# A mixture of experts on one core: whole rows of the weights, contraction outermost over four (two) PSUM banks, bias products first and on 128 rows

## The chip, the core and the metric

The kernel runs on one core of one Trainium2 chip. TensorE (PE) multiplies matrices into PSUM, VectorE (DVE) and ScalarE (ACT) read and write SBUF and PSUM, GpSimd (POOL) does some elementwise work and issues the gathers and scatters, SyncE (SP) issues the loads of the weights. The metric is the device time of one execution in microseconds.

## The reference

The reference is one transformer block (latent attention beside an indexed sparse attention, then a mixture of 32 experts over 512 tokens with 4 experts for each token), followed by two layers of another block. Only the mixture of experts is changed. It is, cut to its core:

```python
logits = xf @ w_router + b_router
top_val, top_idx = lax.top_k(logits, TOP_K)          # 4 of 32 experts for each of 512 tokens
gates = jax.nn.softmax(top_val, axis=-1)
...
def expert_block(args):                              # xb: rows of one expert
    xb, e = args
    hid = xb @ w_mlp1[e] + b_mlp1[e]                 # [1024] x [1024, 2048]
    glu = jnp.minimum(hid[..., ::2], SWIGLU_LIMIT)
    lin = jnp.clip(hid[..., 1::2], -SWIGLU_LIMIT, SWIGLU_LIMIT)
    act = glu * jax.nn.sigmoid(SWIGLU_ALPHA * glu) * (lin + 1.0)
    return act @ w_mlp2[e] + b_mlp2[e]               # [1024] x [1024, 1024]
...
y = y * slot_gate[:, None]
out = jax.ops.segment_sum(y, slot_tok, num_segments=n + 1)[:n]
```

## The kernel before

The function `moe` does the experts one after another, from about 402 to 1660 us of the span. Each expert takes one block of 96 token rows (`NB`), which a gather on POOL brings (`xg`, L967). An expert's weights are 12 MB, loaded in 12 chunks of 1 MB: `load_to` (L937) asks for a chunk of four 128-row tiles by 512 columns, so that a chunk is four pieces of 2 KB for each of the 128 partitions. Eight chunks are of `w_mlp1` (4 column groups, 2 halves of the contraction), four of `w_mlp2` (2 column groups, 2 halves).

Every chunk is split for accuracy: ACT copies it to `whi` (L85), rounded to the format that PE takes at speed, and DVE forms the rest `wlo` = raw - whi (L86). `mm3` (L88 to L92) then makes three products of each 128-row tile: high rows with whi (L90), high rows with wlo (L91), low rows with whi (L92). `split_to` keeps the splits two chunks ahead of the products (`LA`), `load_to` the loads up to five chunks ahead; there are five raw buffers and three pairs of whi and wlo.

`gemm` (L1025) fills one PSUM bank (96 x 512): 24 products over two chunks, and last one product with `bh` and `sel` that adds the bias (L1035). `bh` holds the high parts of the 32 experts' biases in rows 0 to 31 and the low parts in rows 32 to 63; `sel` picks the expert's two rows. The bank `ph` of the first layer has four buffers, the bank `py` of the second two, and a third pair is shared by transposes (`pt`) and the small products `pq` that give the token numbers of a block. After each `ph` bank `swiglu` (L990) runs four DVE operations on 256 columns (`gl` L995, `ln` L997, L998, `act` L999) and one sigmoid on ACT (`sg` L996). The finished activation is transposed on PE (L986) and split into `ah` and `al` for the second layer, which runs one expert late: an expert's turn has the four `ph` banks of expert e and then the two `py` banks of expert e - 1. `index` finds the next rows, `transposed` makes `xh` and `xl` of them. The result `yo` (L1132, ACT) goes to DRAM by a scatter that adds (L1133, POOL).

The order of the instructions on each engine is set by a scheduler from the written order, so the listings below are of the order that it makes. A further loop (`further_blocks`) for experts with more than 96 tokens runs no turn with these inputs.

Of the kernel before, what the change touches and what calls it, by code (L numbers as in the profile page):

```python
# [73 lines left out]
class K:  # L74
# [19 lines left out]
    def rsqrt_mean(self, pool, ss, n, width):  # L94
        """1 / sqrt(ss / n + EPS) for a [P, width] tile."""
# [44 lines left out]
    def build(self):  # L140
        tc = self.tc
        with ExitStack() as ctx:
            E = ctx.enter_context
            self.cp = E(tc.tile_pool(name="consts", bufs=1))
            self.ps = E(tc.tile_pool(name="ps", bufs=1, space=PSUM))
# [5 lines left out]
            with tc.tile_pool(name="cq", bufs=1, side="right", reuse_waits="tile") as self.cq:  # L151
                self.first_block()
                self.hip = E(tc.tile_pool(name="hip", bufs=2, reuse_waits="tile"))
                self.lop = E(tc.tile_pool(name="lop", bufs=2, reuse_waits="tile"))
                if self.upto >= 2:
                    self.moe()
# [14 lines left out]
    def first_block(self):  # L171
# [9 lines left out]
        with tc.tile_pool(name="pjd", bufs=1, reuse_waits="tile") as pjd:  # L181
# [41 lines left out]
            # parameter columns  # L223
# [11 lines left out]
            # shift and scale of the first norm, in columns; normalised x, transposed  # L235
# [38 lines left out]
            # projections; column starts inside w_in  # L274
# [80 lines left out]
    def modrow(self, w, nk=4):  # L355
        """Two rows (to be summed) of cond @ a [1024, 512] piece of w_ada, given in two halves."""
# [12 lines left out]
    def constants_on_chip(self, tmp):  # L369
        """Shape-only constants of the later parts."""  # L370
# [12 lines left out]
        # routing  # L383
# [18 lines left out]
        self.eye2 = cq.tile([64, NE], F32, name="eye2")  # L402
        DVE.tensor_tensor(self.eye2, self.ident[:64, 0:32], self.ident[:64, 32:64], OP.add)
        # per token and expert: chosen or not, 1 + slot (0 if not chosen), (row in tile, tile's first row, 1, gate in three parts)
# [105 lines left out]
    def latent_inputs(self, pq, cl):  # L510
        """Normalised latents, transposed."""
# [71 lines left out]
    def attention_m(self, k1, cl, ym, sel):  # L583
        """Latent attention; the selection and the other modulation rows run beside it."""
# [6 lines left out]
        with ExitStack() as c:  # L591
# [6 lines left out]
            def mods():  # L598
# [4 lines left out]
                # with biases and gains: (gate 1, shift 2, 1 + scale 2, gate 2) of D each  # L603
# [103 lines left out]
    def attention_d(self, qd, kd, vd, ym, dist, modf):  # L707
        """Selected attention with position biases, last query tile first; output projection, residual,
        second norm and router of each finished tile run beside it."""
# [6 lines left out]
        with ExitStack() as c:  # L716
# [17 lines left out]
            def weights(h, j):  # L734
                """Splits of a quarter of the output projection, in two pieces."""
# [38 lines left out]
            def finish(t):  # L774
                """Residual, second norm; the router works on the row before the norm."""
# [11 lines left out]
            def beside():  # L787
# [9 lines left out]
                # shift and scale of the norm go into the router's bias and weights  # L797
# [31 lines left out]
            def router(t, ss):  # L829
# [13 lines left out]
                # the first four of the sorted logits, ties by the lower expert  # L843
# [16 lines left out]
                # gates  # L860
# [51 lines left out]
    def moe(self):  # L912
# [7 lines left out]
        with ExitStack() as c:  # L920
# [6 lines left out]
            # stream of half chunks of weights, in the order of their use  # L927
            seq = []
            for e in range(NE + 1):
                if e < NE:  # L930
                    seq += [(1, e, n, h) for n in range(4) for h in range(2)]
                if e > 0:
                    seq += [(2, e - 1, n, h) for n in range(2) for h in range(2)]
# [3 lines left out]
            def load_to(i):  # L937
                while nxt[0] <= min(i, len(seq) - 1):
                    w, e, n, h = seq[nxt[0]]
                    raws[nxt[0]] = self.wload((w1 if w == 1 else w2)[e], 4 * h, 4, [(512 * n, 512)])  # L940
# [30 lines left out]
            def index(e):  # L971
# [3 lines left out]
                sel = pm.tile([64, NB], F32R, name="sel", bufs=4)  # L975
                ACT.activation(sel, eye2[:, e:e + 1].to_broadcast([64, NB]), AF.Copy)
                return slots(oh, lambda t: vals[:, t, e, :]) + (sel,)

            def transposed(src, hname, nb):
                h = pm.tile([P, KD, NB], F32R, name=hname + "h", bufs=nb)  # L980
                l = pm.tile([P, KD, NB], F32R, name=hname + "l", bufs=nb)
                for g in range(2):
                    pt = self.pb("pt")
                    for k in range(4):
                        kk = 4 * g + k
                        PE.transpose(pt[:, k * NB:(k + 1) * NB], src[:, kk * P:(kk + 1) * P], ident[:NB, :NB])  # L986
                    self.split(h[:, 4 * g:4 * g + 4, :], l[:, 4 * g:4 * g + 4, :], pt[:, :4 * NB].rearrange("p (k n) -> p k n", k=4))
# [744 lines left out]
```

## Time and profile before

| what | value |
|---|---|
| median of 3 runs | 3064.47 us (3064.34 to 3070.38) |
| profiled execution: span | 3067.3 us |
| PE busy | 2922.3 us (95%) |
| DVE busy | 2197.0 us (72%) |
| ACT busy | 1557.6 us (51%) |
| mixture of experts, from its first gather to its end | about 402 to 1660 us |

The profile gives no other time for the profiled execution than its span, which is 2.8 us (0.1%) above the median. The busy time of PE counts matmuls whose ends are modelled, so 95% says that PE hardly waits, not that it works at its peak. The two layers behind the experts (from about 1720 us) are not touched by the change.

### The profile page before, as it was taken

Reading aid. Unit: us, or ns where it says so; the run is one execution under the profiler, and the core shown is the slowest. Engines: PE = TensorE matmul, PEld = TensorE weight load, DVE = VectorE, ACT = ScalarE, POOL = GpSimd, SP = SyncE. Lnnn points to the kernel's source line nnn. Section 1 sums busy time; section 2 is a strip of 40 time slices with the busy share of each in tenths; the row PEclk is TensorE's granted clock in tenths of the full one; section 3 lists DMA queues with packets and bytes.
Section 4 is the critical chain, followed back from the end, with each engine's and each line's share of the span. In section 5 each row is a group of like instructions: output and inputs, shape, how many; then the busy total and the mean of one; then the engine's idle time right before and its main releaser. Section 6 shows DMA issues by size and latency. Waiting matters only on the chain. (4 is left out here: it accounts for less than half of the span.)

```text
span 3067.3 us, 37240 instructions
## 1 busy us (share of the span) xinstructions
PE 2922.3 (95%) x14328; PEld 2183.2 (71%) x14328; DVE 2197.0 (72%) x3370; ACT 1557.6 (51%) x1861; POOL 228.8 (7%) x139
## 2 busy tenths in 40 slices
PE   6999878999999999999996999999999999999998
PEld 4657745666666666666663877888888877888887
DVE  5797787999999999999997576663334576654333
ACT  5475545777777777777765224542223225442222
POOL 1002221111111111111101000000000000000000
PEclk8999979999999999999998999999999999999999
DMA  7243168999999999999997112123332112033330
GB/s 249 89 152 127 56 238 287 341 345 350 350 350 350 350 349 351 347 352 350 348 351 247 56 42 86 42 97 96 96 96 83 56 42 99 28 106 99 98 96 28
DMA packets 314586, 588.63 MB, mean 192 GB/s; under 512 B 16843, under 2 KB 62262, under 8 KB 314406
## 3 DMA queue, kind: packets, MB, share of 16 engines
q1 hardware_dynamic: 303864, 555.63, 52.2%
q0 software_dynamic: 8416, 29.23, 4.0%
q8 instruction: 114, 1.87, 0.3%
q10 hardware_dynamic: 2126, 1.36, 0.1%
q14 instruction: 66, 0.54, 0.1%
HBM read 566.74 MB, written 19.45 MB: 191 GB/s over the span
## 5 line engine op out<-in xcount | busy, mean ns | idle before, releaser
L86 DVE TENSOR_TENSOR wlo<-raw,whi 128x2048 fp32r<-128x2048 f32 (+2 forms) x525 | 1158.5, 2212 | 401.4 <-ACT whi L85 399.9
L85 ACT ACTIVATE whi<-raw 128x2048 fp32r<-128x2048 f32 (+2 forms) x528 | 976.1, 1855 | 579.9 <-PE pa L92 301.0
L90 PE MATMUL ph<-whi,xh 128*96 128x512 f32 x1024 | 415.2, 405 | 10.1 <-issue 8.5
L91 PE MATMUL ph<-wlo,xh 128*96 128x512 f32 x1024 | 411.7, 402 | 2.5 <-DVE wlo L86 2.4
L92 PE MATMUL ph<-whi,xl 128*96 128x512 f32 x1024 | 405.0, 396 | 0.0
L90 PE MATMUL pa<-hh,whi 128*128 128x512 f32 (+1 forms) x808 | 289.6, 359 | 1.3 <-ACT whi L85 1.3
L91 PE MATMUL pa<-hl,whi 128*128 128x512 f32 (+1 forms) x808 | 288.8, 358 | 0.0
L92 PE MATMUL pa<-hh,wlo 128*128 128x512 f32 (+1 forms) x808 | 287.9, 358 | 0.2 <-DVE wlo L86 0.2
L90 PEld LDWEIGHTS ph<-whi,xh 128*96 128x96 f32 x1024 | 166.0, 162 | 100.5 <-issue 34.2
L91 PEld LDWEIGHTS ph<-wlo,xh 128*96 128x96 f32 x1024 | 166.3, 162 | 67.2 <-DVE wlo L86 4.9
L92 PEld LDWEIGHTS ph<-whi,xl 128*96 128x96 f32 x1024 | 166.9, 163 | 64.2
L90 PE MATMUL py<-whi,ah 128*96 128x512 f32 x512 | 206.7, 404 | 1.2 <-ACT ah L85 1.2
L91 PE MATMUL py<-wlo,ah 128*96 128x512 f32 x512 | 205.0, 400 | 0.3 <-DVE wlo L86 0.3
L92 PE MATMUL py<-whi,al 128*96 128x512 f32 x512 | 200.3, 391 | 0.0
L91 PE MATMUL pa<-wlo,uh 128*128 128x512 f32 x512 | 199.3, 389 | 0.0
L92 PE MATMUL pa<-whi,ul 128*128 128x512 f32 x512 | 199.2, 389 | 0.0
L90 PE MATMUL pa<-whi,uh 128*128 128x512 f32 x512 | 199.1, 389 | 0.0
L90 PEld LDWEIGHTS pa<-hh,whi 128*128 128x128 f32 x808 | 154.0, 191 | 26.1 <-ACT z L567 2.2
L92 PEld LDWEIGHTS pa<-hh,wlo 128*128 128x128 f32 x808 | 153.7, 190 | 22.3 <-DVE wlo L86 0.6
L91 PEld LDWEIGHTS pa<-hl,whi 128*128 128x128 f32 x808 | 153.7, 190 | 21.4
L967 POOL DMA_INDIRECT xg<-h2d,ig x32 | 93.3, 2916 | 634.9 <-issue 516.2
L91 PE MATMUL pa<-wlo,hh 128*128 128x512 f32 (+2 forms) x352 | 133.7, 380 | 3.2 <-DVE wlo L86 3.2
(407 smaller groups left out, 4631.5 us busy)
## 6 DMA issues: line engine op xcount, KB each, us to landing
raw<-in_w_mlp SPq DMA_DIRECT2D x384, 1024.0 KB
raw<-in_w_up SPq DMA_DIRECT2D x32, 1024.0 KB
raw<-in_w_down SPq DMA_DIRECT2D x32, 1024.0 KB
raw<-in_w_in SPq DMA_DIRECT2D x26, 1024.0 KB
raw<-in_w_ada SPq DMA_DIRECT2D x24, 1024.0 KB
raw<-in_w_out SPq DMA_DIRECT2D x8, 1024.0 KB
raw<-in_w_o SPq DMA_DIRECT2D x4, 1024.0 KB
acc<-g SPq DMA_DIRECT2D x5, 512.0 KB
```

The lines of the kernel that those rows point to most:

```text
L85: nc.scalar.activation(hi, src, AF.Copy)
L86: (engine or nc.vector).tensor_tensor(lo, src, hi.bitcast(F32), OP.subtract)
L90: mm(out, lh, rh, start=start, stop=False)
L91: mm(out, lh, rl, start=False, stop=False)
L92: mm(out, ll, rh, start=False, stop=stop)
L967: POOL.indirect_dma_start(out=xg, out_offset=None, in_=self.h2d[:, :], in_offset=bass.IndirectOffsetOnAxis(ap=ig[:, :1], axis=0))
```

## The change

The chunks are cut otherwise. A chunk of `w_mlp1` is now 128 whole rows (one piece of 8 KB for each partition), a chunk of `w_mlp2` is 256 whole rows (two pieces of 4 KB); both are still 1 MB, and an expert still has 8 and 4 of them. `gemm` therefore walks over the contraction in its outer loop and writes four banks (`ph`, 96 x 2048) or two (`py`, 96 x 1024) with each tile. Each of these wide tiles has one buffer (4 + 2 banks), and the last two banks are one wide tile `b`, also with one buffer, for `pq`, the transposes and the count of tokens. The bias product comes first, with `bh` and `sel` on 128 rows (rows 64 to 127 of `bh` are set to zero by POOL). `swiglu` works on 1024 columns and is a generator: `gl`, `sg` and `ln` come after the eighth chunk, the other two steps between chunks of the second layer. `yo` is one operation of 1024 columns. The arithmetic is the same apart from the order of the sums.

```diff
-                seq += [(1, e, n, h) for n in range(4) for h in range(2)]
+                seq += [(1, e, k) for k in range(KD)]
...
-                    raws[nxt[0]] = self.wload((w1 if w == 1 else w2)[e], 4 * h, 4, [(512 * n, 512)])
+                    v = self.rawtile().rearrange("p a b -> p (a b)")
+                    if w == 1:
+                        nc.sync.dma_start(v, w1[e][k * P:(k + 1) * P, :])
+                    else:
+                        nc.sync.dma_start(v.rearrange("p (k n) -> p k n", k=2),
+                                          w2[e][k * P:(k + 2) * P, :].rearrange("(k p) n -> p k n", p=P))
...
-                pq = self.pb("pq")
+                pq = wide_bank("b", 2)
...
-                sel = pm.tile([64, NB], F32R, name="sel", bufs=4)
+                sel = pm.tile([P, NB], F32R, name="sel", bufs=4)
...
+            def swiglu(ph, act):
+                v = ph.rearrange("p (f two) -> p f two", two=2)
+                gl = pm.tile([NB, D], F32, name="gl")
+                ln = pm.tile([NB, D], F32, name="ln")
+                sg = pm.tile([NB, D], F32, name="sg")
+                DVE.tensor_scalar(gl, v[:, :, 0], 7.0, None, OP.min)
+                ACT.activation(sg, gl, AF.Sigmoid, scale=1.702)
+                DVE.tensor_scalar(ln, v[:, :, 1], 7.0, -7.0, OP.min, OP.max)
+                yield
+                DVE.scalar_tensor_tensor(ln, ln, 1.0, gl, OP.add, OP.mult)
+                yield
+                DVE.tensor_tensor(act, ln, sg, OP.mult)
...
-            bh = pm.tile([64, 3 * D], F32R, name="bh")
+            bh = pm.tile([P, 3 * D], F32R, name="bh")
+            POOL.memset(bh[64:P, :].bitcast(F32), 0.0)
...
-            def gemm(out, lh, ll, bias, sel):
+            def gemm(out, lh, ll, b0, sel, kt, between):
...
-                    for k in range(4):
-                        kk = 4 * h + k
-                        self.mm3(out, lh[:, kk, :], ll[:, kk, :], wh[:, k, :], wl[:, k, :], kk == 0, False)
+                    between(i)
+                    for k in range(kt):
+                        kk = kt * i + k
+                        for q, (x, w) in enumerate(((lh, wh), (lh, wl), (ll, wh))):
+                            for n in range(nn):
+                                PE.matmul(out[:, 512 * n:512 * n + 512], x[:, kk, :], w[:, nn * k + n, :],
+                                          start=False, stop=kk == KD - 1 and q == 2)
                     pos += 1
-                PE.matmul(out, sel, bias, start=False, stop=True)
...
+                    def between(i):
+                        if i == 2 and e > 0:
                             st[e - 1]["aT"] = transposed(st[e - 1]["act"], "a", 1)
+                        if i == 4 and e + 2 < NE and e != LOOP:
+                            st[e + 2] = dict(zip(("xg", "isc", "gate", "sel"), index(e + 2)))
+                        if i == 6 and e + 1 < NE:
                             st[e + 1]["x"] = transposed(st[e + 1]["xg"], "x", 2)
+                    gemm(ph, s["x"][0], s["x"][1], 0, s["sel"], 1, between)
+                    glu = swiglu(ph, s["act"])
+                    next(glu)
...
-                    for n in range(2):
-                        py = self.py("py")[:NB, :]
-                        gemm(py, s["aT"][0], s["aT"][1], bh[:, F2 + 512 * n:F2 + 512 * n + 512], s["sel"])
-                        ACT.activation(yo[:, 512 * n:512 * n + 512], py, AF.Copy, scale=s["gate"])
+                    py = wide_bank("py", 2)[:NB, :]
+                    gemm(py, s["aT"][0], s["aT"][1], F2, s["sel"], 2, lambda i: next(glu, None))
+                    ACT.activation(yo, py, AF.Copy, scale=s["gate"])
```

In the order of instructions three places change in a way that matters below. The first is DVE at the end of an expert's first layer. Before, the last of the four `ph` banks has its four short operations beside the splits of the chunks (`wlo` is always the split of the next chunk in the stream):

```order
L995 TENSOR_SCALAR gl<-ph 96x256
L997 TENSOR_SCALAR ln<-ph 96x256
L86 TENSOR_TENSOR wlo<-raw,whi 128x2048
L998 SCALAR_TENSOR_TENSOR ln<-ln,gl 96x256
L973 TENSOR_TENSOR oh<-iof_649,rk 128x384
L999 TENSOR_TENSOR act<-ln,sg 96x256
L86 TENSOR_TENSOR wlo<-raw,whi 128x2048 x4
L86 TENSOR_TENSOR al<-pt,ah 128x384 x2
```

Now the whole activation stands there once, and the splits of the second layer's last three chunks stand between its steps. The first piece is the way from the copy of the small products (`sf`) to `gl`; its splits are those of the stream's next four chunks, the last of them the first of the second layer. In the second piece the `wlo` behind `gl` is that of the second of the four chunks of `w_mlp2`, the next two are those of the third and fourth, and the four that follow are those of the next expert's first chunks:

```order
L971 COPY sf<-b 96x6
L86 TENSOR_TENSOR wlo<-raw,whi 128x2048
L974 TENSOR_TENSOR ig<-sf 96x1
L975 TENSOR_REDUCE gate<-sf 96x1
L976 TENSOR_SCALAR sf<-sf,dmp 96x1
L985 TENSOR_TENSOR oh<-iof_649,rk 128x384
L977 SCALAR_TENSOR_TENSOR isc<-sf 96x1
L86 TENSOR_TENSOR wlo<-raw,whi 128x2048 x2
L86 TENSOR_TENSOR xl<-b,xh 128x384
L86 TENSOR_TENSOR wlo<-raw,whi 128x2048
L86 TENSOR_TENSOR xl<-b,xh 128x384
L1012 TENSOR_SCALAR gl<-ph 96x1024
```

Up to `gl` four splits now stand behind the copy `sf` of the small products. The second piece goes on from `gl`:

```order
L1012 TENSOR_SCALAR gl<-ph 96x1024
L86 TENSOR_TENSOR wlo<-raw,whi 128x2048
L1014 TENSOR_SCALAR ln<-ph 96x1024
L86 TENSOR_TENSOR wlo<-raw,whi 128x2048
L1016 SCALAR_TENSOR_TENSOR ln<-ln,gl 96x1024
L86 TENSOR_TENSOR wlo<-raw,whi 128x2048
L1018 TENSOR_TENSOR act<-ln,sg 96x1024
L86 TENSOR_TENSOR wlo<-raw,whi 128x2048 x4
L86 TENSOR_TENSOR al<-b,ah 128x384
```

What moved: one split of a chunk that PE is about to use now stands behind an operation of 1024 columns that waits for the last product of the first layer, and the two after it each behind one more. Between `sf` and `gl` there are four splits, two `xl` and five small operations in a row.

The second place is PE at the change from one layer to the next. Before, each bank ends with its bias product and the next bank, which is another buffer, begins at once:

```order
L92 MATMUL ph<-whi,xl 96x512
L1035 MATMUL ph<-bh,sel 96x512
L986 MATMUL pt<-ident,act 128x96 x4
L90 MATMUL ph<-whi,xh 96x512
L91 MATMUL ph<-wlo,xh 96x512
```

Now the second layer's products follow on the first layer's, and the bias products that open the next expert's `ph` stand among those of the third chunk of the second layer:

```order
L1060 MATMUL ph<-whi,xl 96x512 x4
L1060 MATMUL py<-whi,ah 96x512 x2
L1060 MATMUL py<-wlo,ah 96x512 x2
L1060 MATMUL py<-whi,al 96x512 x2
...
L1060 MATMUL py<-whi,ah 96x512 x2
L1050 MATMUL ph<-bh,sel 96x512 x4
L1060 MATMUL py<-wlo,ah 96x512 x2
```

What moved: the four bias products of `ph` stand together, 13 pairs of products behind the last use of the old `ph`, and what comes behind them on PE waits with them.

The third place is PE at the start of the experts, where before the small products of experts 0 and 1 stand together, and the bias has 24 products ahead of it:

```order
L956 LDWEIGHTS oh
L956 MATMUL pq<-vals,oh 96x6
L986 MATMUL pt<-ident,xg 128x96 x8
L90 MATMUL ph<-whi,xh 96x512
L91 MATMUL ph<-wlo,xh 96x512
L1009 LDWEIGHTS trb
L1009 MATMUL pb<-mk,trb 128x32
```

Now the count, expert 1's small products, its transposes and the bias stand ahead of the first product with weights:

```order
L1003 MATMUL b<-ident,xg 128x96 x8
L1028 LDWEIGHTS trb
L1028 MATMUL b<-mk,trb 128x32
...
L968 LDWEIGHTS oh
L968 MATMUL b<-vals,oh 96x6
L1003 MATMUL b<-ident,xg 128x96 x8
L1050 MATMUL ph<-bh,sel 96x512 x4
L1060 MATMUL ph<-whi,xh 96x512 x4
```

What moved: expert 1's indices and transposes now come one after another through the single tile `b`, and expert 0 waits for all of them. On POOL, whose queue goes in order, both gathers now stand ahead of all loads of the biases, where before two of these loads were ahead of the gathers:

```order
L86 TENSOR_TENSOR wlo<-raw,whi 128x2048 x2
L1035 MEMSET bh 64x3072
L979 DMA xg<-h2d,ig 96x1024 x2
L1039 DMA act<-in_b_mlp 32x1024 x4
L86 TENSOR_TENSOR wlo<-raw,whi 128x2048
L1039 DMA act<-in_b_mlp 32x1024 x2
```

Whatever waits for a load of the biases now also waits for the gather of expert 1.

## Rows read from the trace of the kernel before

**Rows 1.** The page, part 1: busy time of each engine
```profile
PE 2922.3 (95%) x14328; PEld 2183.2 (71%) x14328; DVE 2197.0 (72%) x3370; ACT 1557.6 (51%) x1861; POOL 228.8 (7%) x139
```

**Rows 2.** Windows: busy time in two stretches, granted clock, DMA share, GB/s
```profile
core 0: us, PE busy (x) PEld busy (x) DVE busy (x) ACT busy (x) POOL busy (x), PEclk, DMA share, GB/s
690.00:1570.00 880.00, 880.00 (x3907) 578.39 (x3906) 812.66 (x871) 618.99 (x529) 89.82 (x46) 1.00 1.01 350
440.00:450.00 10.00, 10.00 (x44) 6.38 (x43) 10.00 (x12) 6.54 (x6) 10.00 (x1) 1.00 1.01 363
```

**Rows 3.** The instructions of L1133, the scatter, one an expert, 680 to 1570 us
```profile
L1133 POOL DMA_INDIRECT acc<-yo,isc x24: 1443/1451/1460, 688.4 to 1569.6; - x24
```

**Rows 4.** Groups by line, ten experts, 1000 to 1381 us: busy, mean ns | idle before
```profile
L86 DVE TENSOR_TENSOR wlo<-raw,whi 128x2048 fp32r<-128x2048 f32 x120 | 273.1, 2282 | 18.8 <-ACT whi L85 18.8
L90 PE MATMUL ph<-whi,xh 128*96 128x512 f32 x318 | 128.4, 404 | 0.0
L995 DVE TENSOR_SCALAR gl<-ph 96x256 f32<-96x256 f32 x40 | 16.8, 420 | 9.7 <-PE ph L1035 8.8
L86 DVE TENSOR_TENSOR xl<-pt,xh 128x384 fp32r<-128x384 f32 x20 | 10.9, 546 | 0.0
L973 DVE TENSOR_TENSOR oh<-iof,rk 128x384 bf16<-128x384 f32 x10 | 5.5, 547 | 0.0
L964 DVE TENSOR_SCALAR sf<-sf,dmp 96x1 f32<-96x1 f32 x10 | 2.6, 263 | 0.0
```

**Rows 5.** Timeline of DVE and PE from 1100 us: start, duration, line, operation
```profile
1100.35 4.48 DVE L86 TENSOR_TENSOR wlo<-raw,whi 128x2048 fp32r<-128x2048 f32 x2
1118.09 0.39 PE L90 MATMUL ph<-whi,xh 128*96 128x512 f32 x1
1118.32 0.49 PE L986 MATMUL pt<-ident,xg 96*128 96x96 f32 x4
1118.60 0.45 PE L91 MATMUL ph<-wlo,xh 128*96 128x512 f32 x1
```

**Rows 6.** Timeline of PE from 1146.3 us, at a bias product
```profile
1146.36 0.39 PE L92 MATMUL py<-whi,al 128*96 128x512 f32 x1
1146.68 0.47 PE L1035 MATMUL py<-bh,sel 64*96 64x512 f32 x1
1147.07 0.48 PE L90 MATMUL ph<-whi,xh 128*96 128x512 f32 x1
1147.39 0.40 PE L91 MATMUL ph<-wlo,xh 128*96 128x512 f32 x1
1147.62 0.39 PE L92 MATMUL ph<-whi,xl 128*96 128x512 f32 x1
```

**Rows 7.** Timeline of PE at the start of the experts
```profile
407.31 1.51 PE L986 MATMUL pt<-ident,xg 96*128 96x96 f32 x8 [4.91 <-DMA xg<-h2d,ig]
408.76 0.74 PE L90 MATMUL ph<-whi,xh 128*96 128x512 f32 x1
```

**Rows 8.** Timeline of POOL at the same place
```profile
404.23 1.90 POOL L967 DMA_INDIRECT xg<-h2d,ig  x1 [0.30 <-DVE isc L965]
406.14 2.05 POOL L1019 DMA_DIRECT2D act<-in_b_mlp  x4
```

**Rows 9.** DMA issues, 394 to 412 us: KB each, median us from issue to landing
```profile
act<-in_b_mlp POOLq DMA_DIRECT2D x6, 128.0 KB, 4.3
```

**Rows 10.** The instructions on `bh` up to 500 us: duration ns min/median/max
```profile
L1021 ACT ACTIVATE bh<-act x3: 1039/1041/1057, 399.2 to 415.6; 64x1024 fp32r<-64x1024 f32 x3
L1022 DVE TENSOR_TENSOR bh<-act,bh x3: 1215/1215/1215, 404.1 to 422.4; 32x1024 fp32r<-32x1024 f32 x3
```

**Rows 11.** Waits of the first experts, 400 to 490 us
```profile
PE pt L986 <- DMA xg<-h2d,ig: 8.9, 2, 4.9
PE ph L91 <- DVE wlo L86: 2.2, 2, 1.6
PE ph L90 <- ACT whi L85: 1.6, 2, 1.0
```

More of the change, by code (lines that the diff above doesn't have):

```diff
@@ L151, in build @@
             with tc.tile_pool(name="cq", bufs=1, side="right", reuse_waits="tile") as self.cq:
-                self.first_block()
+                with tc.tile_pool(name="ps", bufs=1, space=PSUM) as self.ps:
+                    self.first_block()
                 self.hip = E(tc.tile_pool(name="hip", bufs=2, reuse_waits="tile"))
@@ L155, in build @@
                 if self.upto >= 2:
-                    self.moe()
+                    with tc.tile_pool(name="psm", bufs=1, space=PSUM) as self.ps:
+                        self.moe()
+                self.ps = E(tc.tile_pool(name="ps2", bufs=1, space=PSUM))
                 h = self.moe_residual()
@@ L925, in moe, with wide_bank @@
             pm = E(tc.tile_pool(name="pm", bufs=1, reuse_waits="tile"))
+            def wide_bank(name, banks):
+                return self.ps.tile([P, 512 * banks], F32, name=name, tag=name)
             seq = []
@@ L930, in moe @@
                 if e < NE:
-                    seq += [(1, e, n, h) for n in range(4) for h in range(2)]
+                    seq += [(1, e, k) for k in range(KD)]
                 if e > 0:
-                    seq += [(2, e - 1, n, h) for n in range(2) for h in range(2)]
+                    seq += [(2, e - 1, k) for k in range(0, KD, 2)]
             raws, sp = {}, {}
@@ L1006, in moe @@
             st[0]["x"] = transposed(st[0]["xg"], "x", 2)
-            pr = self.pb()
+            pr = wide_bank("b", 2)
             for t in range(NT):
@@ L1020, in moe @@
                 js = slice(D * j, D * j + D)
-                ACT.activation(bh[:, js], bl[:64, :], AF.Copy)
+                ACT.activation(bh[:64, js], bl[:64, :], AF.Copy)
                 DVE.tensor_tensor(bh[32:64, js], bl[32:64, :], bh[32:64, js].bitcast(F32), OP.subtract)
             pos = 0
-            def gemm(out, lh, ll, bias, sel):
+            def gemm(out, lh, ll, b0, sel, kt, between):
                 nonlocal pos
-                for h in range(2):
+                nn = 4 // kt
+                for n in range(nn):
+                    PE.matmul(out[:, 512 * n:512 * n + 512], sel, bh[:, b0 + 512 * n:b0 + 512 * n + 512], start=True, stop=False)
+                for i in range(KD // kt):
                     split_to(pos + LA)
                     load_to(pos + 5)
+                    between(i)
                     wh, wl = sp.pop(pos)
-                    for k in range(4):
-                        kk = 4 * h + k
-                        self.mm3(out, lh[:, kk, :], ll[:, kk, :], wh[:, k, :], wl[:, k, :], kk == 0, False)
+                    for k in range(kt):
+                        kk = kt * i + k
+                        for q, (x, w) in enumerate(((lh, wh), (lh, wl), (ll, wh))):
+                            for n in range(nn):
+                                PE.matmul(out[:, 512 * n:512 * n + 512], x[:, kk, :], w[:, nn * k + n, :],
+                                          start=False, stop=kk == KD - 1 and q == 2)
                     pos += 1
-                PE.matmul(out, sel, bias, start=False, stop=True)
             def further_blocks():
@@ L1078, in tr @@
                     def tr(src):
+                        pt = columns(src)
                         for g in range(2):
-                            pt = self.pb("pt")
-                            for k in range(4):
-                                kk = 4 * g + k
-                                PE.transpose(pt[:, k * NB:(k + 1) * NB], src[:, kk * P:(kk + 1) * P], ident[:NB, :NB])
-                            DVE.tensor_copy(xT[:, 4 * g:4 * g + 4, :], pt[:, :4 * NB].rearrange("p (k n) -> p k n", k=4))
+                            DVE.tensor_copy(xT[:, 4 * g:4 * g + 4, :], pt[:, g, :4 * NB].rearrange("p (k n) -> p k n", k=4))
                     def dense(outs, wrows, cols, b0):
@@ L1113, in moe @@
                     s["act"] = pm.tile([P, D], F32, name="act", bufs=2)[:NB, :]
-                    for n in range(4):
-                        ph = self.pa("ph")[:NB, :]
-                        gemm(ph, s["x"][0], s["x"][1], bh[:, 512 * n:512 * n + 512], s["sel"])
-                        swiglu(ph, s["act"], n)
-                        if n == 0 and e > 0:
+                    ph = wide_bank("ph", 4)[:NB, :]
+                    def between(i):
+                        if i == 2 and e > 0:
@@ L1126, in moe @@
+                    glu = swiglu(ph, s["act"])
+                    next(glu)
                 if e > 0:
+                    if e == NE:
+                        st[e - 1]["aT"] = transposed(st[e - 1]["act"], "a", 1)
                     s = st.pop(e - 1)
                     yo = pm.tile([NB, D], F32, name="yo", bufs=2)
-                    for n in range(2):
-                        py = self.py("py")[:NB, :]
-                        gemm(py, s["aT"][0], s["aT"][1], bh[:, F2 + 512 * n:F2 + 512 * n + 512], s["sel"])
-                        ACT.activation(yo[:, 512 * n:512 * n + 512], py, AF.Copy, scale=s["gate"])
+                    py = wide_bank("py", 2)[:NB, :]
```

60 lines of the change are left out of this document (29 added, 31 removed).

## The prediction

> **What bounds the kernel now.** I read the page's totals first: PE is busy 95% of the span, DVE 72%, ACT 51% [rows 1]. Then the windows: between 690 and 1570 us, where the experts follow one another evenly, PE is busy for all of 880.00 us at full clock, and DVE for 812.66 of them [rows 2]. The groups by line say the same: no idle time stands before the products of `ph` [rows 4]. The scatters mark the experts: (1569.6 - 688.4) / 23 = 38.31 us for each [rows 3]. So in this stretch whatever PE issues is the time. But two others are close behind it: DVE with 812.66 / 880 x 38.31 = 35.4 us an expert, and the loads, whose share reads 1.01 at 350 GB/s [rows 2].
>
> What PE's 38.31 us are made of is seen in its timeline. Products start 0.23 us apart (1147.39 to 1147.62). Around a bias product, three steps (1146.36 to 1147.39) take 1.03 us, where three ordinary ones take 0.69 [rows 6]: a bias product on 64 rows costs 0.34 us more than one on 128. An expert has six, 6 x 0.34 = 2.04 us.
>
> **The change, part by part.** The sum is made on the profiled execution, 3067.3 us, and moved to the median by its 2.8 us.
>
> *Bias on 128 rows.* The number of products stays 150 an expert, and the six steps of 64 rows go. I take all of the 2.04 us; if the extra came from the change of bank and not from the rows, none of it would go, and that is the lower end (0). PE alone then needs 38.31 - 2.04 = 36.27 us.
>
> *Wider operations on DVE.* The four steps were 4 x 4 of 0.42 us [rows 4]. For 1024 columns there is one DVE row, the low part of the bias, 1.215 us on 32 partitions [rows 10]. That is also 0.42 us plus three times 256 columns, if a third of the 0.42 is overhead, so I take 1.215; the other end is no gain from width, 4 x 0.42 = 1.68. Neighbours on DVE overlap by 2 x 2.28 - 4.48 = 0.08 us [rows 4, 5], so a step is 1.135 us, and a split 2.20.
>
> *One buffer for `ph`.* Count from the start of the last `ph` product, t = 0. `gl` starts at about 0.5 (its product takes 0.4 [rows 4], and 0.1 is my estimate for the release). Behind it stands the split of the second chunk of `w_mlp2`: 0.5 + 1.135 + 2.28 = 3.9, about 4.0 at PE. PE wants it after 15 steps, 15 x 0.23 = 3.45: **a stall of 0.54 us**, where before PE had none. Then `ln` ends at 5.1, and the next bias products, which wait for `ln` to release `ph`, come behind 13 pairs, after 6.5: no wait. The next two splits end at 7.3 and 10.7; PE wants them at 7.7 and 11.0, so they are in time with 0.4 and 0.3 us to spare. Bounds of this term: 0 (if the release is quicker and PE's first pairs are slower) and 3 x 0.54 = 1.6 (all three late).
>
> *The way to `gl`.* The copy `sf` waits for the small products, which stand in the fifth chunk, and DVE goes in order. Behind it are four splits (8.8 us), two `xl` and `oh` (0.55 each, 1.4 less overlap), and four small ones (0.26 for the longest, about 0.6 in all) [rows 4, 5]: 10.8, with 0.2 for the release 11.0 us until `gl` can start. PE in that time has 42 products (9.7) and eight transposes. Four of them take 0.28 [rows 5], so about 0.6: 10.3 to the end of the last product, 10.6 to `gl` by its start. `gl` comes 0.4 us later than its data, and the stall behind it grows by as much. Bounds 0 and 0.8 (twice the gap, if `sf` is later by a chunk's step).
>
> Together the stall is s = 0.94 us, the expert takes 36.27 + 0.94 = 37.21, which is 1.10 less than before, times 31 turns that have both layers: **-34.1 us**.
>
> *Loads by whole rows.* Same bytes, in larger pieces. At 37.21 us they need 350 x 38.31 / 37.21 = 360 GB/s. The rows reach 363 between 440 and 450 us, where loads catch up [rows 2]. I cost it at nothing; PE's own time covers it, and where that cover goes is a rival below.
>
> *The start.* Now expert 0's first product waits for the single `b` and for POOL's queue. Gather 0 and its transposes end as before, near 408.8 [rows 7]. Their splits (about 1.6, three operations like `xl`), the count, its copy, and expert 1's small products and indices (another 1.6, my estimate) put gather 1 at about 412. It holds POOL for 1.90, four bias loads for 2.05 [rows 8], the last lands 4.3 later [rows 9], and the high and low parts take 1.04 and 1.215 [rows 10]: 422.5, and with the release 422.7 instead of 408.76, +13.9 us. Against that stands that PE idled 4.0 (8.9 less 4.9), 2.2 and 1.6 us in the first experts for a gather and for splits [rows 11], all of which now have 14 us more: -7.8 (bound 0). Expert 0's turn has no second layer, so the bias of expert 1 waits for `gl`, a split and `ln`: about +2.4. In all **+8.5 us** (bounds 6 and 16).
>
> Sum: 3067.3 - 34.1 + 8.5 = 3041.7, by the median **3039 us**.
>
> **The rivals.**
>
> *Slower: the second and third split are late as well.* They have 0.4 and 0.3 us to spare, and the whole chain is DVE's: if `gl`, `ln` and the step after it are each a third of a us longer than 1.215, both come late, and s = 0.94 + 2 x 0.54 = 2.02. Then 31 x (2.02 - 2.04) + 8.5 = +7.9: 3072 us. It decides from s = 2.04 - 8.5 / 31 = 1.77 on. At the far end of 1.68 us for a wide step the walk gives s of about 2.5, or 3087. For it: DVE is already busy 92% of this stretch [rows 2]. Against it: the one row of 1024 columns is 1.215 [rows 10], and the wide steps take 16 x 0.34 - 4 x 1.135 = 0.9 us an expert off DVE. The Trainium skill ("Perfetto Trace Analysis", Optimizing Tensor Performance, Matmuls) says that independent groups should rotate through banks so that evacuation overlaps the next products. This change gives that up for `ph`; by that rule the stall is the larger one. The trace of before, which rotates, shows no idle there, and no run yet shows the other.
>
> *The loads are the bound.* Their share reads 1.01 [rows 2]. If 350 GB/s is all there is, the expert stays at 38.31, the start still costs, and the time is 3064.5 + 8.5 = 3073. Against it: 363 GB/s over 10 us [rows 2], and a PE that never waits. The Trainium skill ("DMA: Bandwidth & Descriptors", Where 436 GB/s comes from) names some 358 GB/s as the limit of one core's HBM share; by that figure the expert's 13.4 MB would take 37.5 us, an estimate from the page. The 363 of the row lies above it.
>
> *No stall.* The splits come in time, because ACT and DVE run ahead or PE's pairs are slower than 0.23 at the start: 36.27 an expert, 3064.5 - 63.2 + 8.5 = 3010.
>
> *The bias gives nothing:* the 0.34 us belong to the change of bank, and the stall stays: +29 + 8.5, 3102. Against it: with four or two banks written in turn there is a change at every product, and then even more would be lost. I give it little.
>
> **How the numbers follow.** The forecast, one late split, 3025 to 3052: 0.45. No or hardly a stall, down to 3010: 0.18. Late splits that eat the gain: 0.18, half of them above 3071. Loads: 0.10. Bias without gain, or something else above 3080: 0.05. The remaining 0.04 lie between 3052 and 3064. A run of this kernel can tell about 0.2% (6 us) from no change. Faster than that: 0.45 + 0.18 + 0.03 = 0.66; within it (3058 to 3071): 0.10, from late splits and loads near the break-even; slower: 0.24. The range 3010 to 3080 leaves out the far ends of both sides, some 0.15. The forecast's own range is 3025 to 3052, from s between 0.5 and 1.3.
>
> **What would show it.** In the profile after: scatters 37.2 us apart; a bias product 0.23 us from its neighbours; one wait of PE for `wlo` of 0.5 to 1 us in each expert, right behind the last product of `ph`, and none at the bias; `gl` of about 1.2 us; the first product with weights near 422 us. I am wrong if PE waits in more than one place of an expert, if PE's step itself is not 0.23, or if the splits wait for landings.

## The result, and the profile after

The changed kernel takes 3032.82 us (median; 3025.86 to 3033.22) against 3064.4 for the kernel before in the same comparison: a ratio of 0.9888, 95% interval 0.9873 to 0.9902. That is 31.6 us less; the forecast was 3039 us, 25.6 less. The profiled executions lie further apart (spans 3067.3 and 3031.2) than the medians, because that of before is its slowest run (3070.38).

The page's first line answers to [rows 1], the windows to [rows 2], the scatters to [rows 3]:

```profile
PE 2867.2 (95%) x14328; PEld 2195.8 (72%) x14328; DVE 2157.9 (71%) x2986; ACT 1540.5 (51%) x1733; POOL 303.4 (10%) x140
```

```profile
700.00:1500.00 800.00, 789.17 (x3660) 551.13 (x3658) 736.72 (x563) 568.59 (x409) 165.46 (x43) 1.00 0.99 361
```

```profile
L1160 POOL DMA_INDIRECT acc<-yo,isc x24: 2538/2554/2571, 722.7 to 1575.5; - x24
```

An expert now takes (1575.5 - 722.7) / 23 = 37.08 us instead of 38.31; 37.21 was forecast. PE, which never waited in this stretch before, is idle for 10.8 of 800 us, the loads run at 361 GB/s instead of 350 and their share fell from 1.01 to 0.99. The granted clock of the stretch is 1.00 as before, though four banks are written in turn. The groups by line of this stretch (busy, mean | idle before) have all of PE's idle time at one place, and the one row that the forecast lacked, an activation step of 1024 columns, is there:

```profile
L1060 PE MATMUL py<-wlo,ah 128*96 128x512 f32 x352 | 111.4, 397 | 10.8 <-DVE wlo L86 10.8
L1012 DVE TENSOR_SCALAR gl<-ph 96x1024 f32<-96x1024 f32 x22 | 26.6, 1210 | 0.1
L1050 PE MATMUL ph<-bh,sel 128*96 128x512 f32 x88 | 23.9, 394 | 0.0
```

`gl` takes 1.210 us, where 1.215 was taken from the bias row [rows 10]. The bias products of `ph` wait for nothing. The timelines of PE and of DVE show one wait (start, duration, operation; "x2" is one operation on two banks):

```profile
1116.15 0.62 PE L1060 MATMUL py<-whi,ah 128*96 128x512 f32 x2
...
1118.92 0.62 PE L1060 MATMUL py<-whi,ah 128*96 128x512 f32 x2
1120.02 0.71 PE L1060 MATMUL py<-wlo,ah 128*96 128x512 f32 x2 [0.48 <-DVE wlo L86]
1120.57 0.62 PE L1060 MATMUL py<-whi,al 128*96 128x512 f32 x2
1121.03 0.62 PE L1060 MATMUL py<-whi,ah 128*96 128x512 f32 x2
```

```profile
1105.79 0.16 DVE L971 COPY sf<-b 96x6 f32<-96x6 f32 x1 [2.51 <-PE b L968]
1105.90 2.29 DVE L86 TENSOR_TENSOR wlo<-raw,whi 128x2048 fp32r<-128x2048 f32 x1
...
1116.09 0.55 DVE L86 TENSOR_TENSOR xl<-b,xh 128x384 fp32r<-128x384 f32 x1
1116.56 1.21 DVE L1012 TENSOR_SCALAR gl<-ph 96x1024 f32<-96x1024 f32 x1
1117.69 2.28 DVE L86 TENSOR_TENSOR wlo<-raw,whi 128x2048 fp32r<-128x2048 f32 x1
1119.89 1.22 DVE L1014 TENSOR_SCALAR ln<-ph 96x1024 f32<-96x1024 f32 x1
```

The wait is the one forecast: the split of the second chunk of `w_mlp2` stands behind `gl`, and PE waits for it after its first pair of that chunk. The idle time in brackets is 0.48 us, but the steps tell more. From 1118.92 to 1120.57 two pairs of products take 1.65 us, where two ordinary pairs take 0.92: the wait costs 0.73 us. An ordinary pair is drawn 0.62 us long and the next starts after 0.46, so the gap that is drawn is shorter than the delay. Before `gl`, DVE works without a gap from `sf` on, as the forecast had it: 1116.56 - 1105.79 = 10.8 us. `gl` starts 0.41 us behind the first product of the second layer (1116.15).

The forecast named splits that wait for landings as a sign of being wrong. ACT, whose copy `whi` comes ahead of the split, waited for no landing in this stretch before. Now it does (total, times, longest wait, 700 to 1500 us):

```profile
ACT whi L85 <- DMA raw<-in_w_mlp: 14.1, 19, 2.0
```

In the turn shown this does not set PE's wait: DVE is busy all the way from `sf` through `gl` to the split that PE waits for.

At the start of the experts PE's timeline answers to [rows 7]:

```profile
408.69 1.51 PE L1003 MATMUL b<-ident,xg 96*128 96x96 f32 x8 [5.72 <-DMA xg<-h2d,ig]
412.54 0.29 PE L1028 MATMUL b<-mk,trb 128*128 128x32 bf16 x4 [2.34 <-DVE xl L86]
...
413.77 1.54 PE L1003 MATMUL b<-ident,xg 96*128 96x96 f32 x8 [0.25 <-DVE sf L971]
416.41 1.14 PE L1050 MATMUL ph<-bh,sel 128*96 128x512 f32 x2 [1.10 <-DVE bh L1042]
419.86 1.17 PE L1050 MATMUL ph<-bh,sel 128*96 128x512 f32 x2 [2.31 <-DVE bh L1042]
420.82 1.91 PE L1060 MATMUL ph<-whi,xh 128*96 128x512 f32 x4
...
425.94 1.11 PE L1060 MATMUL ph<-whi,xh 128*96 128x512 f32 x4
...
449.39 1.58 PE L1050 MATMUL ph<-bh,sel 128*96 128x512 f32 x4 [3.46 <-DVE ln L1014]
```

The first product with weights starts at 420.82 instead of 408.76 us, and the bias of expert 1 waits 3.46 us for `ln`. Yet the first scatter comes only 1.28 us later (before, then after):

```profile
488.71 2.85 POOL L1133 DMA_INDIRECT acc<-yo,isc  x1 [15.25 <-ACT sel L976]
489.99 2.54 POOL L1160 DMA_INDIRECT acc<-yo,isc  x1 [18.06 <-ACT yo L1159]
```

### The profile page after: what moved, and what is told of

Read it like the earlier page. It is cut to its first block, busy times and chain, and to the rows that moved or that the text cites. A ratio compares the mean times of both kernels' runs of the same rounds, so it can differ in the third digit from the quotient of the medians.

```text
span 3031.2 us, 36584 instructions
## 1 busy us (share of the span) xinstructions
PE 2867.2 (95%) x14328; PEld 2195.8 (72%) x14328; DVE 2157.9 (71%) x2986; ACT 1540.5 (51%) x1733; POOL 303.4 (10%) x140
## 5 line engine op out<-in xcount | busy, mean ns | idle before, releaser
L1060 PE MATMUL ph<-whi,xh 128*96 128x512 f32 x1024 | 289.4, 400 | 0.0
L1060 PE MATMUL ph<-wlo,xh 128*96 128x512 f32 x1024 | 289.0, 400 | 0.0
L1060 PE MATMUL ph<-whi,xl 128*96 128x512 f32 x1024 | 280.5, 395 | 0.0
L979 POOL DMA_INDIRECT xg<-h2d,ig x32 | 134.4, 4199 | 426.8 <-issue 367.9
L1060 PE MATMUL py<-wlo,ah 128*96 128x512 f32 x512 | 161.9, 397 | 12.9 <-DVE wlo L86 12.9
L1060 PE MATMUL py<-whi,ah 128*96 128x512 f32 x512 | 160.2, 394 | 0.0
L1060 PE MATMUL py<-whi,al 128*96 128x512 f32 x512 | 159.6, 393 | 0.6 <-DVE al L86 0.6
L1160 POOL DMA_INDIRECT acc<-yo,isc x32 | 81.6, 2549 | 589.2 <-ACT yo L1159 589.2
```

The lines of the kernel that those rows point to most:

```text
L979: POOL.indirect_dma_start(out=xg, out_offset=None, in_=self.h2d[:, :], in_offset=bass.IndirectOffsetOnAxis(ap=ig[:, :1], axis=0))
L1060: PE.matmul(out[:, 512 * n:512 * n + 512], x[:, kk, :], w[:, nn * k + n, :], start=False, stop=kk == KD - 1 and q == 2)
L1160: POOL.indirect_dma_start(out=self.acc[:, :], out_offset=bass.IndirectOffsetOnAxis(ap=s["isc"][:, :1], axis=0), in_=yo, in_offset=None, co ...
```

## The experiments

The theory (A) was that of the prediction: PE is the pace, the steps around 64-row bias products are the gain, and the split behind `gl` takes part of it back. The rivals were that whole rows make the loads faster (B), that the wide activation does it (C), that DVE does not matter (D), and that DVE's whole chain and not the place of one split sets the wait (E).

**One part alone: the bias on 128 rows, on the kernel before.**

```diff
-                sel = pm.tile([64, NB], F32R, name="sel", bufs=4)
-                ACT.activation(sel, eye2[:, e:e + 1].to_broadcast([64, NB]), AF.Copy)
+                sel = pm.tile([P, NB], F32R, name="sel", bufs=4)
+                ACT.activation(sel, eye2[:, e:e + 1].to_broadcast([P, NB]), AF.Copy)
...
-            bh = pm.tile([64, 3 * D], F32R, name="bh")
+            bh = pm.tile([P, 3 * D], F32R, name="bh")
+            POOL.memset(bh[64:P, :].bitcast(F32), 0.0)
```

`eye2` and the copies into `bh` are fitted to this in the same way.

> The kernel before with one part of the change: bh, sel and eye2 on 128 rows, rows 64 to 127 zero. Loads, loops, banks and the four-piece activation are as before. Theory A (the gain is in TensorE's steps around the bias products, and before TensorE was the pace): the expert falls from 38.31 us by 1.5 to 1.9 us to some 36.4 to 36.8, no wait appears, and the time is 3005 to 3020 us, faster than the whole change, since the stall behind ph and the long start are not there. Theory B (loads of 2 KB pieces at 350 GB/s were the limit, and the change gained by whole rows): the expert stays within 0.3 us of 38.31, TensorE now waits for whi and wlo, ACT for landings, and the time is 3055 to 3066 us.

Measured: 3024.79 us, ratio 0.9865 (0.9849 to 0.9882). By the medians this one edit gains more than the whole change, though the two intervals overlap. Its windows and scatters:

```profile
700.00:1500.00 800.00, 799.89 (x3677) 551.09 (x3676) 759.71 (x820) 584.19 (x499) 90.38 (x44) 1.00 1.03 362
```

```profile
L1134 POOL DMA_INDIRECT acc<-yo,isc x24: 1451/1610/1620, 716.1 to 1566.1; - x24
```

PE is still busy throughout, the loads of 2 KB pieces run at 362 GB/s, and the expert takes (1566.1 - 716.1) / 23 = 36.96 us, 1.35 less than before. B falls. The gain is below the 1.5 us that A expected, and the time above its 3005 to 3020 us. PE's timeline shows where most of the rest is:

```profile
1121.07 0.40 PE L92 MATMUL py<-whi,al 128*96 128x512 f32 x1
1121.30 0.39 PE L1036 MATMUL py<-bh,sel 128*96 128x512 f32 x1
1121.53 0.39 PE L90 MATMUL ph<-whi,xh 128*96 128x512 f32 x1
1121.76 0.39 PE L91 MATMUL ph<-wlo,xh 128*96 128x512 f32 x1
...
1146.04 0.39 PE L90 MATMUL py<-whi,ah 128*96 128x512 f32 x1
1146.27 0.33 PE L986 MATMUL pt<-ident,act 96*128 96x96 f32 x2
1146.56 0.47 PE L91 MATMUL py<-wlo,ah 128*96 128x512 f32 x1
```

A bias product now is an ordinary step: 0.69 us for the three steps that took 1.03 [rows 6]. Added up by their starts from 700 to 1500 us, the three steps around each of the six bias products take 4.14 us an expert instead of 6.18, which is the whole 2.04 of the forecast. Part of it comes back elsewhere. Two transposes stood one product behind a bias product and took 0.11 us in the kernel before:

```profile
1141.11 0.33 PE L986 MATMUL pt<-ident,act 96*128 96x96 f32 x2
1141.22 0.45 PE L91 MATMUL py<-wlo,ah 128*96 128x512 f32 x1
```

Now they take 0.29. An expert has two such pairs, and on average they go from 0.11 to 0.28, 0.34 us together; groups of four transposes and the small products cost what they did. The ordinary products start 0.234 us apart instead of 0.232, another 0.28 over 125 of them; why is not shown. PSUM banks are used in this run as before, so the price of the bias product was that of its 64 rows and not of the change of bank.

**One part undone: the bias on 64 rows, in the changed kernel.**

```diff
-                    PE.matmul(out[:, 512 * n:512 * n + 512], sel, bh[:, b0 + 512 * n:b0 + 512 * n + 512], start=True, stop=False)
+                    PE.matmul(out[:, 512 * n:512 * n + 512], sel[:64, :], bh[:64, b0 + 512 * n:b0 + 512 * n + 512], start=True, stop=False)
```

> The changed kernel with the bias products on 64 rows again (first as now, sel and bh cut to rows 0 to 63). Theory A: four steps of ph in a row and two of py; if each 64-row product costs 0.34 us by itself, +2.0 us an expert and some 3090 us; if the cost is that of the switch from 128 to 64 rows and back, a group of four pays it once, +0.6 to +1.0 us an expert, 3050 to 3065 us. Theory B (whole rows): within 5 us of 3033.

Measured: 3051.3 us, ratio 0.9953 (0.9936 to 0.9970).

```profile
L1160 POOL DMA_INDIRECT acc<-yo,isc x24: 2199/2236/2700, 688.5 to 1558.4; - x24
```

```profile
1096.37 0.62 PE L1060 MATMUL py<-whi,ah 128*96 128x512 f32 x2
1096.93 1.15 PE L1050 MATMUL ph<-bh,sel 64*96 64x512 f32 x4
1098.00 0.70 PE L1060 MATMUL py<-wlo,ah 128*96 128x512 f32 x2
1098.54 0.62 PE L1060 MATMUL py<-whi,al 128*96 128x512 f32 x2
```

The expert takes (1558.4 - 688.5) / 23 = 37.82 us, 0.74 more than with 128 rows. The group of four costs (1098.54 - 1096.37) - 8 x 0.23 = 0.33 us more than eight ordinary steps, the same as one such product alone: the price is that of going to 64 rows and back, paid once for a group. Two groups an expert make 0.66 of the 0.74. So the new order of the contraction had already taken most of the six switches away by putting the bias products together.

**Whole rows undone: pieces of 2 KB in the changed kernel.** Each chunk comes by two transfers whose pieces are 2 KB.

```diff
-                        nc.sync.dma_start(v, w1[e][k * P:(k + 1) * P, :])
+                        for c in range(2):
+                            nc.sync.dma_start(v[:, D * c:D * c + D].rearrange("p (a n) -> p a n", a=2),
+                                              w1[e][k * P:(k + 1) * P, :].rearrange("p (a c n) -> p a c n", a=2, c=2)[:, :, c, :])
...
-                                PE.matmul(out[:, 512 * n:512 * n + 512], x[:, kk, :], w[:, nn * k + n, :],
+                                PE.matmul(out[:, 512 * n:512 * n + 512], x[:, kk, :], w[:, (n % 2 * 2 + n // 2) if kt == 1 else 2 * n + k, :],
```

> The changed kernel with each 1 MB chunk loaded by two transfers whose pieces are 2 KB, as before (column blocks swapped in SBUF, the products read them accordingly). All else as in the change. Theory A: the expert stays at about 37.1 us, 3030 to 3040 us, perhaps some late landings. Theory B (whole rows are the gain): the loads fall back to 350 GB/s, the expert goes to about 38.3 us, 3065 to 3075 us.

Measured: 3034.91 us, ratio 0.9898 (0.9881 to 0.9914).

```profile
700.00:1500.00 800.00, 789.08 (x3651) 550.02 (x3650) 736.30 (x558) 571.60 (x409) 166.27 (x43) 1.00 1.04 360
```

The loads run at 360 GB/s as in the change (361), at a share of 1.04 instead of 0.99, and ACT waits 38.4 us for landings instead of 14.1. The time is not told apart from that of the change: whole rows keep the DMA engines less busy and change no time here. B falls a second time.

**The activation in pieces of 256 columns, in the changed kernel.**

```diff
-                DVE.tensor_scalar(gl, v[:, :, 0], 7.0, None, OP.min)
+                cs = [slice(256 * j, 256 * j + 256) for j in range(4)]
+                for j in cs:
+                    DVE.tensor_scalar(gl[:, j], v[:, j, 0], 7.0, None, OP.min)
```

The other three DVE steps are cut in the same way.

> The changed kernel with each of the four VectorE steps of the activation cut into four operations of 256 columns (the sigmoid stays 1024 wide). Theory A: each step takes 4 x 0.34 = 1.36 instead of 1.13 us; the first late split comes 0.23 us later and the next two use up their spare time: stall 0.7 to 1.0 instead of 0.48 us, 3040 to 3050 us. Rival C (the width of the activation is a main part of the gain, because VectorE is as tight as TensorE): 3060 us or more. Rival D (VectorE does not matter): 3033 us.

Measured: 3031.26 us, ratio 0.9882 (0.9865 to 0.9898), as the change. C falls, but not as A expected: the wait did not grow, and PE is idle for 3.7 of 800 us instead of 10.8. The time is the one that D names. DVE's timeline shows that the scheduler put the split between the pieces of `gl`:

```profile
1114.63 0.75 DVE L1014 TENSOR_SCALAR gl<-ph 96x256 f32<-96x256 f32 x2 [0.48 <-PE ph L1065]
1115.31 2.28 DVE L86 TENSOR_TENSOR wlo<-raw,whi 128x2048 fp32r<-128x2048 f32 x1
1117.51 0.74 DVE L1014 TENSOR_SCALAR gl<-ph 96x256 f32<-96x256 f32 x2
```

So the run mixes two effects, dearer steps and a better place, and cannot price the width by itself. For the same reason it does not speak for D: its experts are 36.85 us apart, less than in the change. It suggested the next experiment, which only moves DVE's work.

**The split ahead of `gl`, in the changed kernel.**

```diff
-                DVE.tensor_scalar(gl, v[:, :, 0], 7.0, None, OP.min)
+                with tc.issue_after(after) if after is not None else ExitStack():
+                    DVE.tensor_scalar(gl, v[:, :, 0], 7.0, None, OP.min)
+                    DVE.tensor_scalar(ln, v[:, :, 1], 7.0, -7.0, OP.min, OP.max)
                 ACT.activation(sg, gl, AF.Sigmoid, scale=1.702)
-                DVE.tensor_scalar(ln, v[:, :, 1], 7.0, -7.0, OP.min, OP.max)
```

> The changed kernel, with gl and ln told to stand on VectorE behind the split of the second chunk of the second layer, which PE wants first; nothing else is written otherwise (the scheduler then also moves the small operations of the index a little). Theory A (the 0.48 us that PE waits in each expert are the place of that split behind gl): the wait disappears or falls under 0.15 us, the expert goes from 37.12 to 36.6 to 36.8 us, 3016 to 3023 us. Rival E (VectorE's whole chain is the bound, and the wait only shows where it ends): the wait moves to the bias of ph or to another split, the expert stays at 37.0 to 37.2, 3030 to 3035 us.

Measured: 3022.6 us, ratio 0.9846 (0.9824 to 0.9869). Scatters, and PE's waits from 700 to 1500 us (total, times, longest):

```profile
L1161 POOL DMA_INDIRECT acc<-yo,isc x24: 2102/2695/2723, 723.5 to 1569.3; - x24
```

```profile
PE py L1061 <- DVE wlo L86: 6.9, 24, 0.7
```

The expert falls to (1569.3 - 723.5) / 23 = 36.77 us, and the time to the range that A expected. But 6.9 of the 10.8 us of visible waiting remain, 0.3 an expert where A allowed 0.15. In the timeline PE now waits at the split of the third chunk, which stands behind both `gl` and `ln`. D falls, since work was only moved on DVE. E has a share: the place of the split was the first of DVE's debts, not the only one.

**The index earlier, alone and with the split.** `index` stands between chunks 0 and 1, so that DVE has no small products to wait for late in the turn.

```diff
-                        if i == 4 and e + 2 < NE and e != LOOP:
+                        if i == 1 and e + 2 < NE and e != LOOP:
```

> The changed kernel with the index of the expert after next three chunks earlier (between chunk 0 and 1 instead of 3 and 4), so that VectorE has no small products to wait for in the second half, and gl starts when its data are there. Theory A: gl comes some 0.1 to 0.15 us earlier, the split behind it too, the wait falls from 0.48 to about 0.35, 3027 to 3031 us. Rival E (the chain of small products, four splits and gl sets the wait): it disappears, 3018 us.

> Both edits of order together on the changed kernel: index early, split before gl and ln. Theory A: no wait left, expert 36.6 us, 3015 to 3020 us, the same as with the split alone within 5 us. Rival E: only here, with VectorE relieved at both places, the wait goes; then this is at least 8 us below the split alone.

Measured: 3026.52 us alone, ratio 0.9870 (0.9853 to 0.9886), and 3024.63 with the split, ratio 0.9859 (0.9840 to 0.9877). Alone its interval overlaps that of the change. Two waits from 700 to 1500 us show what it did in the even stretch:

```profile
DVE gl L1012 <- PE ph L1060: 8.5, 12, 1.0
PE py L1060 <- DVE wlo L86: 3.5, 5, 1.0
```

`gl` now waits for its data. In 18 of 22 turns it starts 0.20 us behind the first product of the second layer, where in the change it starts 0.38 to 0.47 behind it in all turns but one: so in the change it was some 0.2 us late. PE's visible wait for the split is gone from these turns (5 are left of 22), and the small products stand in its place. Most experts are some 36.85 us apart instead of 37.11. But a few turns towards the end take 37.4 to 38.6 us, with late splits again, and the mean is 37.03. The first scatter also came earlier (484.29). So neither A's 0.35 us of wait nor E's 3018 us came out.

Together they reach 36.71 us an expert, 0.06 less than the split alone, with 5.0 of 800 us idle. In time the two are not told apart from the split alone, as A expected; its 3015 to 3020 us and "no wait left" were not reached.

**Another start, in the changed kernel.** The biases are asked for first, and expert 1's small products and the count go through the bank of `py`.

```diff
-            st[1] = dict(zip(("xg", "isc", "gate", "sel"), index(1)))
+            st[1] = dict(zip(("xg", "isc", "gate", "sel"), index(1, "py")))
...
-            pr = wide_bank("b", 2)
+            pr = wide_bank("py", 2)
```

> The changed kernel with another start of the experts: biases asked for before the gathers, expert 1's small products and the count in the bank of py instead of b. The steady part is not touched. Theory A (the serial chain through b and POOL's queue costs the start): the first product with weights moves from 420.8 to 410 to 414 us, and the time falls by 4 to 8 us to 3025 to 3029; not by all of the shift, since splits are then not as far ahead. Rival: the splits and loads of the first chunks set the start anyway, first scatter within 1 us of 490.0, 3031 to 3034 us.

Measured: 3021.69 us, ratio 0.9852 (0.9835 to 0.9868). The first product moves to 415.00 us, a little later than expected, the first scatter to 483.66 instead of 489.99; the expert stays at 37.02. The time falls by more than the 4 to 8 us that A expected. The chain through `b` and the order on POOL did cost some 6 us; the run does not tell the two apart.

**Together.**

> The changed kernel with the split before gl and ln (as in e4) and the other start (as in e6). Theory: the two gains are in different stretches and add up: expert 36.8 us, first scatter near 484 us, 3010 to 3016 us, the fastest so far. Rival: TensorE is no longer the bound in either place (VectorE is), and the sum is no better than the better one of the two: 3020 to 3024 us.

> The same with the index early as well. Theory: within 4 us of the run with two edits, since the index alone moved the expert by 0.1 us at most: 3008 to 3016 us. Rival: the early index brings late splits elsewhere (in its own run experts of 37.4 us appeared near the end), 3016 to 3024 us.

Measured: split and start 3018.22 us, ratio 0.9839 (0.9823 to 0.9856); with the index early 3009.48 us, ratio 0.9811 (0.9795 to 0.9827), the fastest of all. The first of the two falls between theory and rival: its start was early (481.95), but its experts took 36.95 us and not the 36.77 of the split alone. The second shows what PE needs when nothing is late; nine of its scatters, and PE's waits in that stretch:

```profile
L1161 POOL DMA_INDIRECT acc<-yo,isc x9: 1571/1676/2525, 1118.6 to 1408.3; - x9
```

```profile
PE ph L1061 <- DVE wlo L86: 0.3, 1, 0.3
```

(1408.3 - 1118.6) / 8 = 36.21 us an expert, with 0.3 us of waiting in eight. Over its whole even stretch it is at 36.60.

## Why the prediction was right, point by point

**What bounds the kernel** held. Taking one cost from PE, and nothing else, made the expert 1.35 us faster with PE busy for 799.89 of 800 us, and loads of the old size followed at 362 GB/s: the rival of the loads falls for this change. The Trainium skill ("DMA: Bandwidth & Descriptors", Where 436 GB/s comes from) gives some 358 GB/s as one core's share of HBM. In the runs with an expert at 37.2 us or less the loads ran at 360 to 366 GB/s over 800 us, a little above it.

**"PE alone then needs 36.27 us"** was right: 36.21 in the stretch without waits. **"I take all of the 2.04 us" for the bias on 128 rows** named the right cause and was incomplete. The first experiment leaves the banks as they were, and the steps around the bias products fall by the 2.04 us; the rival that put the price on the change of bank falls. But there 0.6 us come back at other steps, which leaves 1.35. In the change, 128 rows give only 0.74, since the order of the contraction, costed at nothing on PE in the forecast, by itself leaves two switches of six. That the sum still came near 2.04 is in part luck: the forecast had a row neither for what comes back nor for the order.

**"A stall of 0.54 us" and "`gl` comes 0.4 us later than its data", together s = 0.94:** the single wait stood at the named place and cost 0.73 us an expert in PE's steps, 0.48 of it visible as idle. The 0.54 was right; `gl` was late by 0.2 us and not by 0.4, as the run with the index early shows, and 0.54 + 0.2 comes to the 0.73 measured. The two later splits were in time, as forecast, and so was the bias of `ph` behind its 13 pairs. The expert came out at 37.08 for 37.21. The rule of the Trainium skill ("Perfetto Trace Analysis", Optimizing Tensor Performance, Matmuls) is that independent groups should rotate through banks, so that the emptying of one overlaps the next products. In the even stretch no product waits for the single `ph` itself: the bias products that open it have 0.0 us of idle time before them. What PE waits for is a split that stands behind the emptying on DVE, and 0.31 us an expert came back with `ph` still single when that split was put ahead. Only at the start PE waits for the emptying, 3.46 us.

**The loads at nothing** was right, also with pieces of 2 KB.

**The start, "+8.5 us"**, was the term that was mis-sized, below its own bound of 6. Its pieces came out near the forecast. The first product came 12.06 us later (13.9 forecast), the bias of expert 1 waited 3.46 us (about 2.4 forecast), and the 7.8 us of waits went: 12.06 + 3.46 - 7.8 = 7.7. But the first scatter is only 1.28 us later. One of the 31 turns counted above lies ahead of it, with its gain of 1.2 us, so in the forecast's terms the start cost about 2.5 us. What the forecast left out is known in part. Between the first product with weights and the first scatter there were ten bias products on 64 rows, 10 x 0.34 = 3.4 us, where the forecast counts one turn's 1.1. Twelve transposes and eight small products that stood there, some 1.1 us, now come ahead of that first product or behind the products that the scatter needs. The scatter also follows PE's last product for it some 1 us sooner than before. Against that, three more products, 0.7 us, stand ahead of it. A rest of some 1.5 us is not accounted for.

The clock does not explain it. Before, PE's granted clock was 0.50, the lower of its two levels (1.2 GHz), from 408.76 to 412.56 and from 457.67 to 463.67 us, each time behind a wait for a gather (4.91 and 4.01 us). Now it is 0.50 from 420.82 to 425.94, behind the small products and waits of the start, and 0.61, between the levels, from 449.39 to 453.78, behind the wait of 3.46. Against ordinary steps these spells cost some 4 us in either kernel.

The spans say much the same: 31 x 1.23 = 38.1 us for the experts (34.1 forecast), and the 36.1 us between the two profiled executions leave 2.0 for the start. The forecast, 25.6 us less, was too careful in both terms.

**Of the rivals,** the late splits were the real danger: in the runs with edits of order, waits for `wlo` remain at changing places and PE is idle for 3 to 9 of 800 us. Why the same order of operations runs at 36.21 us in one run's long stretch and at 36.7 in another, with only the start changed, stays open. One candidate is DVE: it is busy for 93% of the time and has little time to catch up once it is late. The other is the loads: in the runs with edits of order, ACT's waits for landings grow from 14.1 us of 800 to between 45.6 and 70.3. In the run with all three edits they are (700 to 1500 us, then 1110 to 1430, the stretch of 36.21):

```profile
ACT whi L85 <- DMA raw<-in_w_mlp: 45.6, 42, 3.1
ACT whi L85 <- DMA raw<-in_w_mlp: 9.4, 11, 2.2
```

So the fast stretch has fewer of them, 9.4 us in 320 against 36.2 in the other 480. In the change SP waits for DVE's splits before it asks for loads (237 times in 800 us), so a late DVE can delay landings as well as the other way round, and no run separates the two. With pieces of 2 KB, landings were waited for 38.4 us and PE's waits stayed as in the change.

## What to carry to other kernels

Look at the steps of the engine that is the pace, not at its busy share: "busy 100%" hid 1.35 us in 38.31 that went with a few lines of zero padding. When a matmul changes the number of rows, group such matmuls or pad them. When an accumulator loses its second buffer, walk the queue of the engine that empties it: the cost is the work that the scheduler puts behind the emptying operation and that the pacing engine needs first, and it can often be put ahead.

## What the runs showed of the hardware

A single matmul on 64 rows between matmuls on 128 costs 0.34 us more than one on 128; four in a row cost 0.33 together. Writing four banks in turn, with each product in another bank than the last, left the granted clock at 1.00 and the step at 0.23 us. A wait of PE shows as 0.48 us idle in the timeline and costs 0.73 in starts. Changing the pieces of the loads from 2 KB to 8 and 4 KB lowered the DMA share from 1.04 to 0.99, at 360 and 361 GB/s.
